# Hybrid decoder step on Trainium2: in the samples' update, the next step's broadcast values are loaded ahead of the state two steps on

## The chip, the cores and the metric

The kernel runs on one core of one Trainium2 chip. Times are device microseconds (us) from the first to the last work of one execution. The engines are TensorE (PE), VectorE (DVE), ScalarE (ACT), GpSimd (POOL) and SyncE (SP). Here POOL does little but issue DMA transfers.

## The reference

One inference step of one layer: a prompt of 256 tokens and 8 samples of one token each, 264 columns in all, model width 2048. The input projection feeds three branches (spatial gating, HGRN2, GLA), which are gated, merged and projected back; a squared-ReLU MLP of width 8192 follows. What matters here is the recurrence of HGRN2 (8 heads, state 128x128) and GLA (4 heads, state 128x256):

```
def gated_linear_recurrence(q, k, v, log_f, s0):
    """S_t = diag(f_t) S_{t-1} + k_t v_t^T ; o_t = S_t^T q_t (per head)."""
    ...
    o = einsum('bhts,bshv->bthv', att, vc) + einsum('bthd,bhdv->bthv', qc * exp(b), S)
    S = exp(b_last)[..., None] * S + einsum('bshd,bshv->bhdv', kc * exp(b_last[:, None] - b), vc)
```

For a sample there is one token: its state comes from DRAM (s0), is scaled by f, gets k v^T added, is multiplied by q, and goes back to DRAM as an output.

## The kernel before

The big products run on PE all the time. The work is cut into granules of 24 matmuls of 128x264 (`granule`): for each of 8 pairs of weight tile and columns, L602 (high part of the weights by high part of the activations), L603 (high by low) and L604 (low by high). The weights come by SP in pieces of 512 KB; ACT casts them to the high part `whi` (L109), DVE subtracts to get the low part `wlo` (L106). Five granules are loaded ahead and two are split ahead. L1296 is an epilogue of such products on DVE.

After each granule `background()` advances a counter `now` and pumps two queues of generators, which write the rest of the layer in small steps between the granules: the mixers of the prompt (`mixer_r`), the updates of the samples (`samples_r`), and others. PE and POOL execute in the order in which this is written. The order of ACT and DVE is set by a scheduler, from the order written and its costs.

`slot()` writes small 32-column matmuls to PE in one entry between two granules: levels of the prompt's recurrence (L633), the samples' output products (L640), and rounds of the conditioning's products (L342). It takes all samples that have waited long enough.

`samples_r(G)` runs for three groups: HGRN heads 0 to 3 (8 steps, one a sample), HGRN heads 4 to 7 (8 steps), and GLA (16 steps, two a sample). In a step

- `fetch` (L1029) has POOL issue the DMA of a state tile `st` (256 KB; 4 buffers). It is called two steps ahead and held back until few enough states are in use; on the chip it also waits until L640 has read the buffer's last content and the write-out L1058 is done.
- `values` (L1035) has POOL issue a broadcast of the step's v rows from the scratch `vs_d` in DRAM (filled by L1086) to all partitions, tile `vbc` (256 KB; 2 buffers). It is called one step ahead.
- ACT scales the state's heads (L1055), DVE adds k times the values (L1057), POOL writes the state out (L1058), and the step is handed to `slot()`, where PE multiplies the state by q (L640; the result `sm` is added to `os`).

A step's work is written when `now` is at least 3 granules past its fetch and 2 past its values (`FETCHED` is 3).

Around it stands `mixer_r` of the same group: L1163 (ACT, an exponential) and L100 (DVE, by q) make `qd`, L1165 makes `kd`, L1176 multiplies the two on PE, L1188 transposes `kd` on PE, L1189 copies the result by ACT to `kt`, L1197 and L1198 multiply that by v on PE, L1201 scales the result and L1203 writes it out by POOL; L1220, L1222 and L1223 make outputs on PE, L1225, L1228 and L1234 treat them on ACT, and L1243 transposes them on PE.

Of the kernel before, what the change touches and what calls it, by code (L numbers as in the profile page):

```python
# [57 lines left out]
def hybrid_step_kernel(  # L58
# [27 lines left out]
    def blk(shape=None, dt=F32):  # L86
        shape = shape or [P, 4, NT]
        return blkp.tile(shape, dt, tag="b", name=nm("b"))
# [4 lines left out]
    def tmp(shape, tag, bufs=2):  # L93
        return tp.tile(shape, F32, tag=tag, name=nm(tag), bufs=bufs)
# [4 lines left out]
    def mul(o, a, b):  # L99
        V.tensor_tensor(o, a, b, op=ALU.mult)  # L100
# [72 lines left out]
    def rstd_small(ms, scale, out):  # L173

        n, w = out.shape
        xx, aa = tmp([P, 16], "sx")[0:n, 0:w], tmp([P, 16], "sa")[0:n, 0:w]
        c = 0
        for m in ms if isinstance(ms, list) else [ms]:
            V.tensor_scalar(xx[:, c:c + m.shape[1]], m, scale, EPS, ALU.mult, ALU.add)
            c += m.shape[1]  # L180
        V.tensor_scalar(out.bitcast(I32), xx.bitcast(I32), -0.5, 1597463007.0, ALU.mult, ALU.add)
        for _ in range(3):
            mul(aa, out, out)
            V.scalar_tensor_tensor(aa, aa, -0.5, xx, ALU.mult, ALU.mult)
            V.scalar_tensor_tensor(out, aa, 1.5, out, ALU.add, ALU.mult)
# [828 lines left out]
    def samples_r(G):  # L1014

        dv = G.dv
        nj, nh = dv // P, 512 // dv
        q, k, g = G.q, G.k, G.g
        fs = tmp([P, 4, NS], "fs")
        S.activation(fs, g[:, :, NP:NT], AF.Exp)  # L1020
        qm = blk([P, 4, NS, 32])
        mul(qm, q[:, :, NP:NT].unsqueeze(3).to_broadcast([P, 4, NS, 32]),
            delta.rearrange("p (b c) -> p b c", b=NS).unsqueeze(1).to_broadcast([P, 4, NS, 32]))
        steps = [(b, h) for b in range(NS) for h in range(0, 4, nh)]
        ahead, vals = [], []

        def fetch(b, h):
            st = tmp([P, nh, dv], "st", ST_BUFS)
            nc.gpsimd.dma_start(st, G.s_in(b, h, nh))  # L1029
            ahead.append((st, now[0]))  # L1030

        def values(b, h):
            v = tmp([P, 4, P], "vbc", VB_BUFS)
            r0 = 4 * nj * b + h * nj
            nc.gpsimd.dma_start(v, vs_d[G.i, r0:r0 + 4, :].partition_broadcast(P))  # L1035
            vals.append((v.rearrange("p (h j) v -> p h (j v)", h=nh), now[0]))

        for s in steps[0:2]:
            fetch(*s)
            yield  # L1040
        values(*steps[0])
        yield
        os_ = tmp([P, dv], f"os{G.i}", 1)
        sts = []
        for n, (b, h0) in enumerate(steps):
            if n + 2 < len(steps):

                yield lambda: len(sts) + sum(len(x[3]) for x in samples) <= ST_BUFS - 3
                fetch(*steps[n + 2])
            if n + 1 < len(steps):  # L1050
                values(*steps[n + 1])
            yield lambda: now[0] >= max(ahead[0][1] + FETCHED, vals[0][1] + FETCHED - 1)
            st, v = ahead.pop(0)[0], vals.pop(0)[0]
            for i in range(nh):
                S.activation(st[:, i, :], st[:, i, :], AF.Copy, scale=fs[:, h0 + i, b:b + 1])  # L1055
            for i in range(nh):
                V.scalar_tensor_tensor(st[:, i, :], v[:, i, :], k[:, h0 + i, NP + b:NP + b + 1], st[:, i, :], ALU.mult, ALU.add)  # L1057
            nc.gpsimd.dma_start(G.s_out(b, h0, nh), st)  # L1058
            sts.append(st)
            if h0 + nh == 4:  # L1060
                samples.append((now[0], (G, qm, os_), b, sts))
                sts = []
            yield
        yield lambda: not samples
        yield READY
        ss, rr = tmp([P, 1], "sss", 1), tmp([P, 1], "srr", 1)
        S.activation(tmp([P, dv], "vt"), os_, AF.Square, accum_out=ss)
        rstd_small(ss, 1.0 / dv, rr)
        S.activation(os_, os_, AF.Copy, scale=rr)
        G.os = os_  # L1070
        yield

    def mixer_r(G):
# [18 lines left out]
        q, k, g = G.q, G.k, G.g  # L1092

        bs.g.append(samples_r(G))


# [333 lines left out]
    for m in range(7):  # L1430
        if m in PRE_AT:
            n = N_PRE // len(PRE_AT)
# [387 lines left out]
```

## Time and profile before

| | |
|---|---|
| median of 3 runs | 1940.19 us (1938.92 to 1940.46) |
| profiled execution | 1938.0 us, span 1935.8 us |
| mean granted PE clock | 0.995 |
| PE busy | 1900.1 us, 98% of the span |
| DVE busy | 1188.7 us, 61% |
| ACT busy | 1005.7 us, 52% |
| POOL busy | 88.0 us, 5% |
| DMA | 442.06 MB, mean 228 GB/s |

A row of a group gives line, engine, operation, output <- inputs, shapes and count. A row of the waits reads "who waited <- for whom: us in total, times, longest us". A row of the timeline gives start and length in us, then the instruction, and in brackets how long its engine had been idle before it and what ended that. A matmul's length overlaps that of the next, so the pace of PE is read from the starts. A row of the windows gives the busy time of each engine in a stretch, and the clock that PE was granted in it (1.00 is full speed). The three groups of samples lie at about 380 to 520, 520 to 660 and 660 to 860 us.

### The profile page before, as it was taken

The page shows a single profiled execution, that of the slowest core. Times are in us where ns is not written, and L with a number is a line of the kernel's source. Part 1 is how long each engine was busy: PE and PEld are TensorE (multiplying, and loading weights), DVE is VectorE, ACT ScalarE, POOL GpSimd, SP SyncE. Part 2 cuts the span into 40 slices and gives each one's busy share as a digit, 9 for nine tenths or more (in the row PEclk, how much of TensorE's full clock was granted, in tenths as well). Part 3 has the DMA queues.
Part 4 walks back from the last instruction along what each step waited for, and adds up shares of the span by engine and source line. Part 5 has one row for each costly group of instructions (what it writes and reads, how often), then busy time and mean ns, then how long its engine had stood idle before and what let it go on. Part 6 is the DMA issues. An engine that isn't in the chain of part 4 may idle for free. (4 is left out here: it accounts for less than half of the span.)

```text
span 1935.8 us, 42323 instructions
## 1 busy us (share of the span) xinstructions
PE 1900.1 (98%) x17072; PEld 1810.3 (94%) x17072; DVE 1188.7 (61%) x2114; ACT 1005.7 (52%) x1827; POOL 88.0 (5%) x144
## 2 busy tenths in 40 slices
PE   6999999999999999999999999999999999999998
PEld 5989999998999998999999989999999999999997
DVE  4566667686577695565555666545556555555565
ACT  5444354665666765544444566454444545454444
POOL 1000000001101112200000010000000000000000
PEclk9999999999999999999999999999999999999999
DMA  9897787688588788987777846776565555555552
GB/s 314 299 341 250 246 285 216 212 259 277 182 268 280 220 261 277 312 262 250 253 256 231 304 138 191 226 243 191 180 184 178 184 179 181 183 178 185 179 181 100
DMA packets 339381, 442.06 MB, mean 228 GB/s; under 512 B 14931, under 2 KB 281025, under 8 KB 339185
## 3 DMA queue, kind: packets, MB, share of 16 engines
q1 hardware_dynamic: 329120, 409.62, 65.5%
q0 software_dynamic: 8992, 28.48, 4.6%
q8 instruction: 134, 2.20, 0.4%
q10 hardware_dynamic: 1072, 1.25, 0.2%
q14 instruction: 63, 0.51, 0.1%
HBM read 427.60 MB, written 11.70 MB: 227 GB/s over the span
## 5 line engine op out<-in xcount | busy, mean ns | idle before, releaser
L602 PE MATMUL mm<-b,whi 128*128 128x264 f32 x4592 | 1317.2, 287 | 7.6 <-ACT b L109 3.5
L603 PE MATMUL mm<-b,whi 128*128 128x264 f32 x4592 | 1308.6, 285 | 1.9 <-DVE b L106 1.0
L604 PE MATMUL mm<-b,wlo 128*128 128x264 f32 x4592 | 1305.3, 284 | 0.3 <-DVE wlo L106 0.2
L106 DVE TENSOR_TENSOR wlo<-raw,whi 128x512 fp32r<-128x512 f32 x1136 | 776.0, 690 | 570.0 <-ACT whi L109 567.4
L109 ACT CAST whi<-raw 128x512 fp32r<-128x512 f32 x1134 | 693.9, 618 | 726.7 <-PE mm L603 647.9
L602 PEld LDWEIGHTS mm<-b,whi 128*128 128x128 f32 x4592 | 865.8, 189 | 50.2 <-issue 23.8
L603 PEld LDWEIGHTS mm<-b,whi 128*128 128x128 f32 x4592 | 865.8, 189 | 2.6 <-DVE b L106 1.1
L604 PEld LDWEIGHTS mm<-b,wlo 128*128 128x128 f32 x4592 | 866.3, 189 | 1.4 <-DVE wlo L106 0.9
L103 DVE TENSOR_TENSOR b<-b,mm 128x528 f32<-128x528 f32 (+1 forms) x137 | 95.6, 699 | 42.3 <-PE mm L604 42.3
L1057 DVE SCALAR_TENSOR_TENSOR st<-vbc,b,st 128x128 f32<-128x128 f32 (+1 forms) x96 | 34.2, 391 | 52.3 <-DMA vbc<-vs_d 46.8
L1055 ACT ACTIVATE st<-st,fs 128x128 f32<-128x128 f32 (+1 forms) x96 | 37.0, 430 | 51.3 <-DMA st<-in_state_hgrn_dram 26.0
L274 PE MATMUL ada<-b,cT 128*32 128x256 f32 (+1 forms) x640 | 35.4, 361 | 7.4 <-DMA b<-in_w_ada_dram 7.3
L342 PE MATMUL ada<-araw,cT 128*32 128x512 f32 x296 | 39.9, 601 | 0.0
L274 PEld LDWEIGHTS ada<-b,cT 128*32 128x32 f32 x640 | 18.3, 116 | 19.5 <-issue 6.8
L100 DVE TENSOR_TENSOR b<-b,b 128x512 f32<-128x512 f32 (+1 forms) x47 | 34.2, 742 | 1.4 <-ACT b L1165 0.9
L1058 POOL DMA_DIRECT2D out_dram<-st x32 | 23.5, 735 | 153.1 <-DVE st L1057 152.3
L342 PE MATMUL ada<-b,cT 128*32 128x512 f32 x216 | 25.8, 593 | 0.0
L106 DVE TENSOR_TENSOR b<-gt,b 128x528 fp32r<-128x528 f32 x32 | 22.7, 709 | 3.7 <-ACT whi L109 0.5
L106 DVE TENSOR_TENSOR b<-b 128x1024 f32<-128x1024 f32 (+1 forms) x24 | 24.4, 1018 | 0.0
L109 ACT CAST whi<-araw 128x512 fp32r<-128x512 f32 x20 | 12.4, 621 | 20.6 <-PE mm L603 18.1
L100 DVE TENSOR_TENSOR gt<-vt 128x528 f32<-128x528 f32 x32 | 22.4, 701 | 0.9 <-ACT vt L1679 0.9
L1685 ACT ACTIVATE b<-vt 128x528 fp32r<-128x528 f32 x32 | 20.7, 647 | 1.0
(374 smaller groups left out, 872.0 us busy)
## 6 DMA issues: line engine op xcount, KB each, us to landing
raw<-in_w_in_dram SPq DMA_DIRECT2D x232, 512.0 KB, 4.6
raw<-in_w_mlp_up_dram SPq DMA_DIRECT2D x128, 512.0 KB, 3.7
raw<-in_w_mlp_down_dram SPq DMA_DIRECT2D x128, 512.0 KB, 3.6
b<-in_w_ada_dram SPq DMA_DIRECT2D x102, 512.0 KB, 6.5
araw<-in_w_ada_dram SPq DMA_DIRECT2D x74, 512.0 KB, 5.4
raw<-in_w_branch_dram SPq DMA_DIRECT2D x48, 512.0 KB, 4.4
raw<-in_w_out_dram SPq DMA_DIRECT2D x32, 512.0 KB, 4.1
b<-in_w_ada_dram SPq DMA_DIRECT2D x32, 256.0 KB, 5.9
```

The source lines that it names most:

```text
L100: V.tensor_tensor(o, a, b, op=ALU.mult)
L103: V.tensor_tensor(o, a, b, op=ALU.add)
L106: V.tensor_tensor(o, a, b, op=ALU.subtract)
L109: S.copy(hi, src)
L274: T.matmul(acc[32 * j:32 * j + 32, 0:n], cT[:, k, :], w[:, n * j:n * j + n], start=k == 0, stop=k == KT - 1)
L342: T.matmul(self.acc[32 * j:32 * j + 32, :], cT[:, k, :], ws[j // 2][:, j % 2 * 512:j % 2 * 512 + 512], start=k == 0, stop=k == KT - 1)
L602: T.matmul(o, a, xh(k + j), start=first and j == 0, stop=False)
L603: T.matmul(o, a, xl(k + j), start=False, stop=False)
L604: T.matmul(o, b, xh(k + j), start=False, stop=last and j == n - 1)
L1055: S.activation(st[:, i, :], st[:, i, :], AF.Copy, scale=fs[:, h0 + i, b:b + 1])
L1057: V.scalar_tensor_tensor(st[:, i, :], v[:, i, :], k[:, h0 + i, NP + b:NP + b + 1], st[:, i, :], ALU.mult, ALU.add)
L1058: nc.gpsimd.dma_start(G.s_out(b, h0, nh), st)
```

## The change

In each step of `samples_r`, the call of `values` for the next step is made ahead of the condition that holds back the fetch, and ahead of the fetch; before, it was made behind both.

```
         for n, (b, h0) in enumerate(steps):
+            if n + 1 < len(steps):
+                values(*steps[n + 1])
             if n + 2 < len(steps):
 
                 yield lambda: len(sts) + sum(len(x[3]) for x in samples) <= ST_BUFS - 3
                 fetch(*steps[n + 2])
-            if n + 1 < len(steps):
-                values(*steps[n + 1])
             yield lambda: now[0] >= max(ahead[0][1] + FETCHED, vals[0][1] + FETCHED - 1)
```

On POOL this is the end of the first group. Names are tiles with numbers: st are the states of steps 4 to 7 (fetched here: before 5842, 5855, 6097 and after 5844, 5857, 6099 are steps 5, 6 and 7), vbc the values.

```order
-L1029 DMA st_5842<-in_state_hgrn_dram 128x4x128
-L1035 DMA vbc_5844<-vs_d 128x512
-L1058 DMA out_dram<-st_5455 128x4x128
-L1029 DMA st_5855<-in_state_hgrn_dram 128x4x128
-L1035 DMA vbc_5857<-vs_d 128x512
-L1058 DMA out_dram<-st_5602 128x4x128
-L1029 DMA st_6097<-in_state_hgrn_dram 128x4x128
-L1035 DMA vbc_6099<-vs_d 128x512
-L1058 DMA out_dram<-st_5842 128x4x128
 L1035 DMA vbc_6110<-vs_d 128x512
```
```order
+L1035 DMA vbc_5683<-vs_d 128x512
+L1029 DMA st_5844<-in_state_hgrn_dram 128x4x128
+L1058 DMA out_dram<-st_5457 128x4x128
+L1035 DMA vbc_5855<-vs_d 128x512
+L1029 DMA st_5857<-in_state_hgrn_dram 128x4x128
+L1058 DMA out_dram<-st_5604 128x4x128
+L1035 DMA vbc_5950<-vs_d 128x512
+L1029 DMA st_6099<-in_state_hgrn_dram 128x4x128
+L1058 DMA out_dram<-st_5844 128x4x128
 L1035 DMA vbc_6110<-vs_d 128x512
```

Each vbc issue has moved ahead of the st issue before it, so a step's values now precede the fetch of the state one step later. The last one, vbc_6110 of step 7, has no fetch to pass and keeps its place behind the write-out of step 5.

On DVE this is the stretch that ends with the L100 for which L1176 of the first group waits. Before (st_5855 is step 6, st_6097 is step 7):

```order
L100 TENSOR_TENSOR b_6088<-b_6088,b_4812 128x1024
L106 TENSOR_TENSOR wlo_6079<-raw_5937,whi_6078 128x512
L1057 SCALAR_TENSOR_TENSOR st_5855<-vbc_6099,b_4812,st_5855 128x128 x3
L106 TENSOR_TENSOR wlo_6083<-raw_5937,whi_6082 128x512
L1057 SCALAR_TENSOR_TENSOR st_5855<-vbc_6099,b_4812,st_5855 128x128
L1057 SCALAR_TENSOR_TENSOR st_6097<-vbc_6110,b_4812,st_6097 128x128 x2
L106 TENSOR_TENSOR wlo_6141<-raw_5982,whi_6140 128x512
L1057 SCALAR_TENSOR_TENSOR st_6097<-vbc_6110,b_4812,st_6097 128x128
L1296 SCALAR_TENSOR_TENSOR b_5863<-gt_6051,mm_6053 128x528
L106 TENSOR_TENSOR wlo_6145<-raw_5982,whi_6144 128x512
L1057 SCALAR_TENSOR_TENSOR st_6097<-vbc_6110,b_4812,st_6097 128x128
L106 TENSOR_TENSOR wlo_6177<-raw_6016,whi_6176 128x512
```

After (st_6099 is step 7; b_6091 in L100 is `qd`):

```order
L100 TENSOR_TENSOR b_6090<-b_6090,b_4812 128x1024
L106 TENSOR_TENSOR wlo_6081<-raw_5946,whi_6080 128x512
L1057 SCALAR_TENSOR_TENSOR st_6099<-vbc_6110,b_4812,st_6099 128x128 x2
L106 TENSOR_TENSOR wlo_6085<-raw_5946,whi_6084 128x512
L1057 SCALAR_TENSOR_TENSOR st_6099<-vbc_6110,b_4812,st_6099 128x128 x2
L106 TENSOR_TENSOR wlo_6150<-raw_5984,whi_6149 128x512
L100 TENSOR_TENSOR b_6091<-b_6091,b_170 128x512
L1296 SCALAR_TENSOR_TENSOR b_5872<-gt_6053,mm_6055 128x528
```

Step 6's adds have moved up (they stand further ahead now), and one L106 and the L1296 no longer stand between step 7's first add and the L100 of `qd`, which before follows the last row shown.

On PE the samples' products of steps 5 and 6 of the first group are now in one entry. After:

```order
L604 MATMUL mm_6160<-b_1274,wlo_6085 128x264
L633 MATMUL sm_6245<-b_5909 32x64 x16
L640 MATMUL sm_6262<-st_5844,b_5016 32x128
L640 MATMUL sm_6262<-st_5857,b_5016 32x128
L640 MATMUL sm_6262<-st_5844,b_5016 32x128
```

Before, the entry behind L633 holds step 5 alone (st_5842), step 6 has the next entry with L1188 and L342, and step 7 one of its own later. In the whole program PE has three entries with 32-column matmuls fewer; the number of matmuls is the same.

On ACT, in the third group, the copies to `kt`. Before:

```order
L109 CAST whi_10110<-raw_9957 128x512
L109 CAST whi_10114<-raw_9957 128x512
L1189 COPY b_10124<-sm_10125 128x512
L1189 COPY b_10124<-sm_10131 128x512
L109 CAST whi_10161<-raw_10013 128x512
```

After (st_10096 and st_10152 are steps 8 and 9):

```order
L1189 COPY b_10089<-sm_10090 128x512
L1055 ACTIVATE st_10096<-st_10096,fs_9007 128x256
L1055 ACTIVATE st_10152<-st_10152,fs_9007 128x256
L109 CAST whi_10134<-raw_9973 128x512
L1055 ACTIVATE st_10152<-st_10152,fs_9007 128x256
L109 CAST whi_10138<-raw_9973 128x512
L1189 COPY b_10089<-sm_10144 128x512
```

The scaling of two more states has moved in between the two copies. In this group PE's entries with L640 stand up to 8 granules earlier than before, the last one behind granule 219 instead of 227.

More of the change, by code (lines that the diff above doesn't have):

```diff
@@ L1045, in samples_r @@
         for n, (b, h0) in enumerate(steps):
+            if n + 1 < len(steps):
+                values(*steps[n + 1])
             if n + 2 < len(steps):
@@ L1049, in samples_r @@
                 fetch(*steps[n + 2])
-            if n + 1 < len(steps):
-                values(*steps[n + 1])
             yield lambda: now[0] >= max(ahead[0][1] + FETCHED, vals[0][1] + FETCHED - 1)
```

## The prediction

> **What bounds the kernel now.** I read the totals of the page first, then the list of waits, then PE's own waits in the stretch where the samples are updated, then the timeline around the one wait found there.
>
> ```profile
> span 1935.8 us, 42323 instructions
> PE 1900.1 (98%) x17072; PEld 1810.3 (94%) x17072; DVE 1188.7 (61%) x2114; ACT 1005.7 (52%) x1827; POOL 88.0 (5%) x144
> ...
> POOL st L1029 <- PE sm L640: 132.3, 12, 17.8
> ...
> DVE st L1057 <- DMA vbc<-vs_d: 46.8, 18, 5.9
> ...
> ACT st L1055 <- DMA st<-in_state_gla_dram: 25.0, 10, 6.8
> ```
>
> PE is busy for 98% of the span, so a wait costs time only where PE ends up idle. The waits that the change aims at are long (DVE waited 18 times for broadcast values, 46.8 us), but DVE is busy 61% and ACT 52%. How much of them reaches PE is told by PE's waits from 380 to 520 us (first HGRN group) and by its busy time per stretch (columns: stretch, length, PE, PEld, DVE, ACT and POOL busy, granted clock, DMA share, GB/s; the last row sums 380 to 860 us, all three groups):
>
> ```profile
> PE sm L1176 <- DVE b L100: 3.8, 1, 3.8
> PE mm L604 <- DVE wlo L106: 0.2, 1, 0.2
> ...
> 380.00:520.00 140.00, 136.01 (x1526) 125.23 (x1519) 94.14 (x188) 87.99 (x190) 14.56 (x22) 0.99 0.77 249
> ...
> sum 480.00, PE 475.62 PEld 442.88 DVE 328.04 ACT 302.86 POOL 66.86; mean PE 118.91 PEld 110.72 DVE 82.01 ACT 75.71 POOL 16.71
> ```
>
> In those 480 us PE is idle 480.00 − 475.62 = 4.38 us, and 3.99 of it lies in the first group: nearly all one wait, L1176 for L100. That is the only place where the 46.8 us can be seen on the path, and the whole gain has to come from there and from how PE's pieces are cut. Its surroundings:
>
> ```profile
> 478.77 1.16 PE L1176 MATMUL sm<-b,b 128*128 128x128 f32 x8 [3.76 <-DVE b L100]
> ...
> 480.57 0.42 PE L604 MATMUL mm<-b,wlo 128*128 128x264 f32 x1
> ...
> 483.21 0.42 PE L604 MATMUL mm<-b,wlo 128*128 128x264 f32 x1
> ...
> 483.73 0.29 PE L604 MATMUL mm<-b,wlo 128*128 128x264 f32 x1
> ...
> 484.10 0.28 PE L604 MATMUL mm<-b,wlo 128*128 128x264 f32 x1
> ```
> ```profile
> 474.37 0.61 DVE L1057 SCALAR_TENSOR_TENSOR st<-vbc,b,st 128x128 f32<-128x128 f32 x2 [0.35 <-DMA vbc<-vs_d]
> 474.90 0.69 DVE L106 TENSOR_TENSOR wlo<-raw,whi 128x512 fp32r<-128x512 f32 x1
> 475.50 0.34 DVE L1057 SCALAR_TENSOR_TENSOR st<-vbc,b,st 128x128 f32<-128x128 f32 x1
> 475.77 0.70 DVE L1296 SCALAR_TENSOR_TENSOR b<-gt,mm 128x528 f32<-128x528 f32 x1
> 476.38 0.68 DVE L106 TENSOR_TENSOR wlo<-raw,whi 128x512 fp32r<-128x512 f32 x1
> 476.98 0.34 DVE L1057 SCALAR_TENSOR_TENSOR st<-vbc,b,st 128x128 f32<-128x128 f32 x1
> 477.25 0.68 DVE L106 TENSOR_TENSOR wlo<-raw,whi 128x512 fp32r<-128x512 f32 x1
> 478.03 0.69 DVE L100 TENSOR_TENSOR b<-b,b 128x512 f32<-128x512 f32 x1
> ```
> ```profile
> 477.36 0.63 ACT L1163 ACTIVATE b<-b 128x512 f32<-128x512 f32 x1 [1.87 <-DVE st L1057]
> ```
>
> Read backwards: PE (idle from 478.77 − 3.76 = 475.01) waits for L100, L100 for the exponential L1163, L1163 for the last add L1057 of the group's last step, and the first of those adds waited for its broadcast values until 474.37. The values left POOL last in a burst of four:
>
> ```profile
> 465.48 0.75 POOL L1029 DMA_DIRECT2D st<-in_state_hgrn_dram  x1 [0.21 <-PE sm L640]
> 466.22 0.55 POOL L1035 DMA_DIRECT2D vbc<-vs_d  x1
> 466.76 0.76 POOL L1058 DMA_DIRECT2D out_dram<-st  x1
> 467.51 0.55 POOL L1035 DMA_DIRECT2D vbc<-vs_d  x1
> ```
>
> Issued at 467.51, they were used at 474.37, 6.86 us later.
>
> **The change part by part.** It swaps two issues on POOL in 6 of the 8 steps of each HGRN group and 14 of the 16 of the GLA group; nothing is added or dropped, and POOL is busy 88 us in all, so issuing itself costs nothing. The values no longer stand behind the fetch that waits for a state buffer (132.3 us of waits for PE's L640, above). The price is that each fetch is issued one values issue later, 0.55 us. No new blocking: the buffer of the next values needs the adds of the step before last, and the write-out just ahead on POOL already waits for those.
>
> *The stall at L1176.* The values of the last step keep their place, behind the write-out of step 5. But those of step 6 leave the burst, being issued a wave earlier; step 7's are then third of three. The fetch still waits for L640 of step 3, which stands in the same row of PE, so the issues are at 465.48, 466.2 and 467.0: 0.52 us earlier (467.51 − 466.99). Fewer transfers lie ahead; step 6's, second in its burst, landed within 6.07 us, from 466.22 to the add that did not wait for it:
>
> ```profile
> 472.29 0.87 DVE L1057 SCALAR_TENSOR_TENSOR st<-vbc,b,st 128x128 f32<-128x128 f32 x3
> ```
>
> With that, the last values are there at 466.99 + 6.07 = 473.1, that is 1.3 us earlier. Behind them DVE's order is shorter: one L106 (476.38) and the L1296 (475.77) no longer stand between the last adds and L1163, 0.60 + 0.61 = 1.2 us by their start-to-start times. Together −2.5; the stall shrinks from 3.76 to about 1.2. Bounds: −1.2 (only the order) and −3.76 (all of it). I take −2.5.
>
> *The clock behind it.* The granted clock falls in stretches of 3.41 us:
>
> ```profile
> 104.66:108.07 3.41, 1.39 (x12) 1.20 (x11) 3.37 (x9) 1.97 (x4) 0.00 (x0) 1.00 0.80 253
> 108.07:111.48 3.41, 3.41 (x18) 3.41 (x17) 2.11 (x8) 1.78 (x3) 0.00 (x0) 0.50 1.04 392
> ```
> ```profile
> 473.30:476.71 3.41, 1.71 (x15) 1.50 (x13) 3.06 (x8) 1.08 (x2) 0.76 (x1) 1.00 1.07 403
> 476.71:480.12 3.41, 1.35 (x11) 1.35 (x12) 2.51 (x5) 1.24 (x3) 0.76 (x1) 1.00 1.04 393
> 480.12:483.54 3.42, 3.42 (x18) 3.42 (x17) 0.69 (x1) 1.11 (x2) 0.00 (x0) 0.50 0.90 329
> ```
>
> Where PE was busy 1.39 or 1.35 of 3.41 us, the next stretch ran at clock 0.50; after 1.71 it did not. At half clock twelve matmuls took 483.21 − 480.57 = 2.64 us, 0.22 each; at full clock three took 484.10 − 483.73 = 0.37, 0.123 each. 3.42 / 0.22 = 15.5 matmuls, each 0.097 late: 1.5 us. A stall that ends near 476.2 leaves 476.71 to 480.12 busy, so I take −1.5 (bounds 0 and −1.5; the stretches may lie otherwise in other executions). The Trainium skill, "TensorE: Matmul & The Clock Gate", section "Why this matters for your kernels", asks for no PE-idle gaps over about 3 us. By it a residual stall of up to 3 us would be free of the clock's loss; by the stretch from 104.66, where 3.41 − 1.39 = 2.02 us of idleness was enough, it would not. The 3.76 us agree with the rule, the 2.02 us don't, and the measurement decides; at 1.2 us both give −1.5.
>
> *PE's pieces.* The products L640 of two steps now go to PE in one entry more often: three entries with 32-column matmuls fewer, the same matmuls. What entering and leaving costs:
>
> ```profile
> 784.87 0.28 PE L604 MATMUL mm<-b,wlo 128*128 128x264 f32 x1
> 785.08 0.64 PE L640 MATMUL sm<-st,b 128*32 128x256 f32 x8
> 785.65 0.39 PE L602 MATMUL mm<-b,whi 128*128 128x264 f32 x1
> 785.88 0.28 PE L603 MATMUL mm<-b,whi 128*128 128x264 f32 x1
> ```
>
> 785.08 − 784.87 = 0.21 and 785.88 − 785.65 = 0.23 against 0.12 inside the stream: 0.2 us an entry, −0.6 for three. Bounds 0 and, if the whole 785.88 − 784.87 − 0.24 = 0.77 went, −2.3.
>
> *The third group.* Its steps come closer together (L640 entries up to 8 granules earlier), so states are fetched sooner after their buffers come free and ACT, which scales them, has less slack. One place touches PE: the copy L1189 that L1198 needs stands behind step 9's L1055 now. Such a state took this long before:
>
> ```profile
> 803.11 0.72 POOL L1029 DMA_DIRECT2D st<-in_state_gla_dram  x1 [8.32 <-PE sm L640]
> ```
> ```profile
> 809.56 0.91 ACT L1055 ACTIVATE st<-st,fs 128x256 f32<-128x256 f32 x2 [6.79 <-DMA st<-in_state_gla_dram]
> ```
> ```profile
> DMA to landing us min/median/max: 3.0/5.7/9.5
> ```
>
> That is 6.45 us from issue to use, and ACT's 6.79 us there cost PE nothing; over all states (last row) the slowest took 9.5. The new place is in no row of before. Bounds: −0.4, all that PE idles outside the first group (4.38 − 3.99), and +4.5, if a state lands at 9.5 instead of 6.45, L1198 waits all of the 3.0 us between and the clock's 1.5 go too. The median of 5.7 lies below the 6.45 that cost nothing, so I take a value near the lower end, +0.2. The 0.2 us at L604 above, behind a late L106, goes: −0.2.
>
> Sum: −2.5 − 1.5 − 0.6 + 0.2 − 0.2 = −4.6 us. The profiled execution took 1938.0 us (span 1935.8 plus 2.2), so the profile after should read about 1933.4; the median of the runs, 1940.19, lies 2.2 above it, and 1940.19 − 4.6 = 1935.6.
>
> **The rivals.**
> 1. *The third group gives it back*: step 9's state lands late, L1198 waits up to those 3.0 us and the clock may fall. For it: ACT waited 10 times, up to 6.8 us, for these states. Against: none of those waits reached PE. Instead of +0.2 there stand +3.0 or +4.5: −1.8 or −0.3, 1938.4 to 1939.9.
> 2. *The stall stays*, because the values of the last step are not moved ahead of any fetch: they land as late as before, some 6.9 us after issue, or L1163 has another wait in its place, so that only order and pieces gain, and the clock still falls: −0.6 for the pieces alone to −1.2 − 0.6 = −1.8: 1938.4 to 1939.6. For it: the row at 467.51 stands in the same place in both programs; against: the burst ahead of it gets shorter.
> 3. *Slower*: each fetch stands 0.55 us later behind a 256 KB broadcast, and in the third group six pairs of steps follow on one another more tightly. If states then land towards 9.5 us after issue, ACT stands in L1055 with the casts L109 of the weights behind it, and PE starves once a pair. It decides from 1.5 us a pair, half of the 3.0 above: 6 × 1.5 = 9.0, less 4.6, is +4.4: 1944.6. Against: before, ACT stood still for 6.79 us without a gap on PE.
>
> The Trainium skill, "SBUF — State Buffer", section "SBUF: two separate sides", warns that DMAs issued from POOL starve for descriptors while DVE runs some of its operations; that would work towards rival 3, as DVE's work gets denser. The four issues at 465.48 to 467.51 took 0.55 to 0.76 us each in a busy stretch; no row shows one held up.
>
> **How the numbers follow.** My forecast has 0.60 (own range 1932.6, the larger bounds of pieces and stall, to 1937.5), rival 1 0.17, rival 2 0.13, rival 3 0.10. A measurement of this kernel tells about 0.2%, 3.9 us, from no change, so faster means below 1936.3. Of the forecast's 0.60 I put 0.46 below that; 0.02 of rival 1 too: faster 0.48. The rest of the forecast, of rival 1 and rival 2 give 0.42 for the same; slower 0.10. The range from 1932.6 to 1941.0 leaves out rival 3 and as much again for costs that no row bounds.
>
> **What would show it.** PE's wait at L1176 of the first group near 1.2 us, at most 2.5; no stretch at clock 0.50 behind it; DVE's waits for the values well under 46.8 us, most of this without effect; the last values issued about 467.0 and used by 473.1; PE idle from 660 to 860 us still under 0.5 us. Wrong, if L1176 still waits over 3 us, or if L1198, L1220 or L1243 wait on ACT, or L602 to L604 on L109 or L106, in the third group.

## The result, and the profile after

The changed kernel is slower by 0.3%: 1947.05 us (median of 18 runs) against 1940.63 us for the kernel before (18 runs). The ratio is 1.0029, 95% interval 1.0020 to 1.0038; of 1940 us that is +5.6 us (+3.9 to +7.4). It is not the ratio of the medians, and it leaves out one slow run of the kernel before, of 2063.71 us. Below, each ratio is turned into us in the same way. The profiled execution took 1948.27 us, 1.2 above its median; the one of before, 1938.0, lay 2.6 below its own, so the two profiles lie further apart than the kernels do.

The page and the waits of the changed kernel:

```profile
span 1946.0 us, 42329 instructions
PE 1904.0 (98%) x17072; PEld 1812.8 (93%) x17072; DVE 1189.5 (61%) x2113; ACT 1004.1 (52%) x1827; POOL 87.7 (5%) x144
...
DVE st L1057 <- DMA vbc<-vs_d: 32.7, 13, 5.8
```

The change did what it says to the wait it is aimed at: DVE waited 32.7 us for values instead of 46.8. PE, however, now waits in all three groups (its waits from 380 to 520, from 520 to 660 and from 660 to 860 us, and then the sum row of the windows 380 to 520, 520 to 660 and 660 to 865 us):

```profile
PE sm L1176 <- DVE b L100: 1.9, 1, 1.9
PE mm L604 <- DVE wlo L106: 0.9, 1, 0.9
...
PE sm L633 <- DVE b L100: 2.1, 1, 2.1
PE mm L604 <- DVE wlo L106: 1.0, 1, 1.0
...
PE sm L1198 <- ACT b L1189: 2.1, 1, 2.1
PE sm L1243 <- ACT b L1245: 1.2, 1, 1.2
PE mm L604 <- DVE wlo L106: 0.9, 1, 0.9
...
sum 485.00, PE 473.91 PEld 440.08 DVE 325.98 ACT 297.55 POOL 66.11; mean PE 157.97 PEld 146.69 DVE 108.66 ACT 99.18 POOL 22.04
```

PE is idle 485.00 − 473.91 = 11.09 us there, against 4.38 before. One wait was halved and six came in its place. I lined the two executions up by the start of every 24th big matmul. The first group then gained 1.0 us, the second lost 5.2 and the third 7.0. That is one pair of executions; the experiments give each group by itself.

**First group, its start.** The values of the fourth step were issued at 411.20, and DVE was there long before they landed (POOL, DVE and PE, in the timeline):

```profile
411.20 0.55 POOL L1035 DMA_DIRECT2D vbc<-vs_d  x1
...
419.88 1.14 DVE L1057 SCALAR_TENSOR_TENSOR st<-vbc,b,st 128x128 f32<-128x128 f32 x4 [1.56 <-DMA vbc<-vs_d]
420.94 0.68 DVE L106 TENSOR_TENSOR wlo<-raw,whi 128x512 fp32r<-128x512 f32 x1
...
421.67 0.39 PE L604 MATMUL mm<-b,wlo 128*128 128x264 f32 x1 [0.90 <-DVE wlo L106]
```

DVE stands 1.56 us for values issued 8.68 us before, does four adds, and only then the low part that PE needs. In DVE's order of before, these adds stood a whole wave later, and the same low part followed on the last add of the third step:

```profile
418.42 0.34 DVE L1057 SCALAR_TENSOR_TENSOR st<-vbc,b,st 128x128 f32<-128x128 f32 x1
418.68 0.69 DVE L106 TENSOR_TENSOR wlo<-raw,whi 128x512 fp32r<-128x512 f32 x1
```

The scheduler has put the fourth step's adds ahead of `wlo` because their DMA now stands earlier on POOL: with the order of the DMAs changed alone (the first experiment below) they stand there too, and with the writing times changed alone they do not.

**First group, L1176.** (POOL, ACT, DVE, PE, then the busy time and the clock of two stretches.)

```profile
467.42 0.55 POOL L1035 DMA_DIRECT2D vbc<-vs_d  x1
...
472.51 1.12 ACT L109 CAST whi<-raw 128x512 fp32r<-128x512 f32 x2
...
474.21 0.61 DVE L1057 SCALAR_TENSOR_TENSOR st<-vbc,b,st 128x128 f32<-128x128 f32 x2 [1.44 <-ACT whi L109]
...
477.39 1.16 PE L1176 MATMUL sm<-b,b 128*128 128x128 f32 x8 [1.93 <-DVE b L100]
...
475.13:478.55 3.42, 1.50 (x13) 1.28 (x13) 3.32 (x8) 2.18 (x4) 0.76 (x1) 1.00 1.03 396
478.55:481.96 3.41, 3.41 (x19) 3.41 (x18) 1.69 (x4) 1.20 (x2) 0.00 (x0) 0.51 0.87 278
```

The stall fell from 3.76 to 1.93 us. The last values were again used 6.8 us after their issue (467.42 to 474.21). The row names L109 as what ended DVE's wait, but those casts were done at 473.63; by the trace the values landed at 474.13, so it was they. And 1.93 us of idleness was enough for half clock in the next stretch (0.51).

**Second group.** Before, PE did not wait here. Now the adds of step 4 wait on DVE for values that left POOL 9.3 us earlier, and an L100 that the level products L633 need stands behind them; half clock follows (POOL, DVE, PE and the clock after, then DVE before):

```profile
579.53 0.55 POOL L1035 DMA_DIRECT2D vbc<-vs_d  x1
...
588.83 0.35 DVE L1057 SCALAR_TENSOR_TENSOR st<-vbc,b,st 128x128 f32<-128x128 f32 x1 [5.82 <-DMA vbc<-vs_d]
...
591.04 0.95 PE L633 MATMUL sm<-b 128*32 128x32 f32 x64 [2.14 <-DVE b L100]
...
591.26:594.68 3.42, 3.42 (x81) 3.04 (x68) 3.42 (x8) 0.00 (x0) 1.04 (x2) 0.50 0.71 178
```
```profile
585.59 0.62 DVE L1057 SCALAR_TENSOR_TENSOR st<-vbc,b,st 128x128 f32<-128x128 f32 x2 [1.80 <-DMA vbc<-vs_d]
```

Before, the adds of step 3 stood at this place and waited 1.80 us, for values that had left POOL second in their burst, behind a fetch alone. The values of step 4, which are needed there now, leave third, behind a fetch and a write-out: 9.3 us from issue to use instead of 6.5 (579.12 to 585.59).

**Third group.** The steps come earlier, so state 9 is fetched at 750.03. Its scaling stands on ACT ahead of the second copy L1189, for which PE's L1198 waits:

```profile
750.03 0.70 POOL L1029 DMA_DIRECT2D st<-in_state_gla_dram  x1
...
758.47 0.51 ACT L1055 ACTIVATE st<-st,fs 128x256 f32<-128x256 f32 x1 [2.31 <-DMA st<-in_state_gla_dram]
...
760.31 0.57 ACT L1189 COPY b<-sm 128x512 f32<-128x512 f32 x1
...
760.94 0.70 PE L1198 MATMUL sm<-b,b 128*128 128x256 f32 x2 [2.07 <-ACT b L1189]
...
762.02:765.44 3.42, 3.42 (x16) 3.25 (x15) 2.54 (x5) 0.91 (x3) 0.58 (x1) 0.51 0.82 238
...
805.95 0.66 PE L1243 MATMUL sm<-cst,b 128*128 128x128 f32 x4 [1.25 <-ACT b L1245]
```

State 9 landed about 8.4 us after its issue (750.03 to 758.47). In the kernel before the two copies stood together and waited for no state:

```profile
749.61 1.07 ACT L1189 COPY b<-sm 128x512 f32<-128x512 f32 x2
```

### The profile page after: what moved, and what is told of

Same layout as the page of the kernel before. It is cut to its first block, busy times and chain, and to the rows that moved or that the text cites. A ratio compares the mean times of both kernels' runs of the same rounds, so it can differ in the third digit from the quotient of the medians.

```text
span 1946.0 us, 42329 instructions
## 1 busy us (share of the span) xinstructions
PE 1904.0 (98%) x17072; PEld 1812.8 (93%) x17072; DVE 1189.5 (61%) x2113; ACT 1004.1 (52%) x1827; POOL 87.7 (5%) x144
## 5 line engine op out<-in xcount | busy, mean ns | idle before, releaser
L604 PE MATMUL mm<-b,wlo 128*128 128x264 f32 x4592 | 1306.6, 285 | 3.0 <-DVE wlo L106 2.8
L106 DVE TENSOR_TENSOR wlo<-raw,whi 128x512 fp32r<-128x512 f32 x1136 | 777.0, 690 | 588.3 <-ACT whi L109 586.0
L109 ACT CAST whi<-raw 128x512 fp32r<-128x512 f32 x1134 | 693.1, 618 | 727.6 <-PE mm L603 651.8
L604 PEld LDWEIGHTS mm<-b,wlo 128*128 128x128 f32 x4592 | 867.1, 189 | 5.1 <-DVE wlo L106 4.5
L1057 DVE SCALAR_TENSOR_TENSOR st<-vbc,b,st 128x128 f32<-128x128 f32 (+1 forms) x96 | 33.9, 391 | 41.7 <-DMA vbc<-vs_d 32.7
L342 PE MATMUL ada<-araw,cT 128*32 128x512 f32 x296 | 40.9, 600 | 0.2 <-DMA araw<-in_w_ada_dram 0.2
L274 PEld LDWEIGHTS ada<-b,cT 128*32 128x32 f32 x640 | 18.4, 116 | 19.0 <-issue 6.8
L100 DVE TENSOR_TENSOR b<-b,b 128x512 f32<-128x512 f32 (+1 forms) x47 | 34.1, 743 | 1.2 <-ACT b L1165 0.9
L342 PE MATMUL ada<-b,cT 128*32 128x512 f32 x216 | 27.5, 627 | 0.0
L106 DVE TENSOR_TENSOR b<-gt,b 128x528 fp32r<-128x528 f32 x32 | 22.7, 708 | 3.4
L106 DVE TENSOR_TENSOR b<-b 128x1024 f32<-128x1024 f32 (+1 forms) x24 | 24.4, 1019 | 0.0
L109 ACT CAST whi<-araw 128x512 fp32r<-128x512 f32 x20 | 12.4, 622 | 20.9 <-PE mm L603 19.1
L100 DVE TENSOR_TENSOR gt<-vt 128x528 f32<-128x528 f32 x32 | 22.4, 701 | 0.9 <-ACT vt L1679 0.9
L342 PEld LDWEIGHTS ada<-b,cT 128*32 128x32 f32 x216 | 7.2, 114 | 16.4 <-issue 16.0
```

The lines of the kernel that those rows point to most:

```text
L106: V.tensor_tensor(o, a, b, op=ALU.subtract)
L109: S.copy(hi, src)
L274: T.matmul(acc[32 * j:32 * j + 32, 0:n], cT[:, k, :], w[:, n * j:n * j + n], start=k == 0, stop=k == KT - 1)
L342: T.matmul(self.acc[32 * j:32 * j + 32, :], cT[:, k, :], ws[j // 2][:, j % 2 * 512:j % 2 * 512 + 512], start=k == 0, stop=k == KT - 1)
L604: T.matmul(o, b, xh(k + j), start=False, stop=last and j == n - 1)
```

## The experiments

The change does two things at once. It changes the order of the DMAs on POOL, and it changes when a step's work is written: the rule "3 granules after the fetch of the state, 2 after the values" was bound by the values, and these are now issued before the hold. In the edits below, `ahead_of` selects the steps whose values go ahead of the fetch; where it is false the order is that of before. Line numbers in the experiments are shifted by a few (L1057 is then L1059, L1060 or L1062, and so on).

### Order and pace taken apart, all groups

The order alone (the DMAs of after, the writing times of before), against the changed kernel:

```
                 fetch(*steps[n + 2])
+            if n + 1 < len(steps):
+                vals[-1] = (vals[-1][0], now[0])
```

> The DMAs stand as in the changed kernel, but a step's work (scaling, adds, products) is written at the granule at which the kernel before writes it: the time of the values' issue is taken where it was before, behind the fetch. PE's pieces stand as before. Theory A (most of the loss comes from the steps being written up to some granules earlier, so that their instructions stand in ACT's and DVE's order before their data has landed): the waits of the third group (L1198, L1243) and the 2.1 us at L633 of the second are gone, the three waits of 0.9 to 1.0 us of L604 at the start of each group stay, since DVE's adds of the fourth step still stand there, and L1176 still gains 1.8: between -1 and +3 us against the kernel before. Rival B (the transfers' order alone costs: a state issued behind a broadcast lands later): as the changed kernel, +5 to +7 us.

Measured: 1.0034 (1.0021 to 1.0046), +6.6 us.

The pace alone (the DMAs of before, the writing times of after), against the kernel before:

```
+            seen = now[0]
             if n + 2 < len(steps):
...
                 values(*steps[n + 1])
+                vals[-1] = (vals[-1][0], seen)
```

> The DMAs stand in the order of the kernel before, but a step's work is written as early as in the changed kernel: the time of the values' issue is taken ahead of the hold. PE's pieces stand as in the changed kernel. Theory A: +3 to +5 us against the kernel before; L1198 and L1243 of the third group wait 1 to 2 us each, L1176 of the first group still waits about 3.8 us, and L604 does not wait at the start of the groups. Rival B: within 1 us of the kernel before.

Measured: 1.0043 (1.0029 to 1.0057), +8.3 us. Neither theory held for both: the order alone came out where rival B had it, the pace alone above both. By the point values each half alone costs no less than both together, so they are not two terms of a sum. On the waits theory A was mostly right. With the order alone there was none at L1198 and L1243, but the 2.0 us at L633, which it saw gone, stayed, and L604 waited 1.2 us in the second and the third group and only 0.2 in the first; with the pace alone L1198 and L1243 waited 1.7 and 2.0 us and L1176 3.9 us.

Lined up with the kernel before by the big matmuls, as above, these two profiled executions split by group: the order alone gained 2.6 us in the first group and lost 4.6 in the second and 1.8 in the third; the pace alone lost 0.5, 0.2 and 8.5. So the gain at L1176 (2.0 us of wait with the order alone) and the loss of the second group go with the order, and most of the loss of the third group with the pace. Each is one execution.

### One group at a time

```
+            ahead_of = G.i < 2      # or: G.i == 2, G.i == 1, G.i == 0
```

> The change in the two HGRN groups alone, the GLA group as before. From the drift between the two profiled executions (+1.4 at the start of the first group, -2.3 around L1176, +1.3 and +3.7 in the second) theory A gives +2 to +4 us. A rival C, that all of the loss sits in the third group, gives -2 to 0.

Measured: 1.0001 (0.9992 to 1.0009), +0.2 us (−1.6 to +1.7): below theory A's 2 to 4, at the edge of rival C's −2 to 0.

> The change in the GLA group alone. From the drift (+1.5 at its start, and some +5 to +6 from L1198 on): theory A gives +3 to +6 us; rival C +6 to +8, all of the loss and the gain of the first group missing too; if the loss were in the HGRN groups, 0 to +1.

Measured: 1.0026 (1.0016 to 1.0036), +5.0 us, of about 5.6 in all, as theory A had it and less than rival C. In its profiled execution L1198 waits 1.4 us and L1243 1.3, and no stretch of the clock halves there, so some 2.7 of the 5.0 us are named and the rest is not. So the third group holds nearly all of the net loss. That the HGRN groups net nothing is no sign that nothing happens there:

> The change in the second HGRN group alone. If the HGRN groups' loss sits here: L604 waits 0.9 to 1.2 us at the group's start and L633 waits 1.6 to 2.1 us for L100, behind adds that wait for values: +3 to +5 us against the kernel before. Rival (the loss sits at the start of the first group): +1 to +1.5 us, the wait of L604 alone.

Measured: 1.0020 (1.0011 to 1.0029), +3.9 us, with the two waits expected, one of them longer:

```profile
PE mm L604 <- DVE wlo L106: 2.2, 1, 2.2
PE sm L633 <- DVE b L100: 1.7, 1, 1.7
```

> The change in the first HGRN group alone, from its first step on. It differs from the run of the group's tail by the values of steps 1 to 3 alone. If the second group holds the loss: -3 to -5 us, the gain of the tail less the wait of L604 at the start. Rival: -1 to +1 us, the start taking back what the tail brings.

Measured: 0.9979 (0.9970 to 0.9988), −4.1 us. First, second and third group give −4.1 + 3.9 + 5.0 = +4.8 us, inside the interval of the whole (+3.9 to +7.4): the account closes by group. That the first group's −4.1 is near the −4.6 of the forecast is luck: in its profiled execution L1176 still waited 2.0 us and a stretch at half clock followed, so of the forecast's terms the clock's did not come and the stall's came in part.

### Order and pace in the third group

The same two edits as above, for `G.i == 2` alone.

> In the GLA group alone: the DMAs in the changed order, a step's work written at the granule at which the kernel before writes it. Theory A in the third group (its loss comes from steps written earlier: L1198 and L1243 behind the scaling of states that have not landed, and the rounds L342 shifted): no wait at L1198 and L1243, at most the wait of about 1 us of L604 seen in the run with the DMA order alone: 0 to +2 us against the kernel before. Rival B: the +4.9 us of the GLA group come from the DMA order: +4 to +6.

Measured: 1.0004 (0.9996 to 1.0012), +0.8 us.

> In the GLA group alone: the DMAs in the order of the kernel before, but a step's work written as early as in the changed kernel. Theory A: L1198 and L1243 wait 1 to 2 us each: +4 to +8 us against the kernel before (the run with this in all groups gave +8.3). Rival B: within 1 us of it.

Measured: 1.0044 (1.0030 to 1.0058), +8.5 us. PE's waits from 660 to 870 us:

```profile
PE sm L1246 <- ACT b L1248: 2.9, 1, 2.9
PE sm L1201 <- ACT b L1192: 2.1, 1, 2.1
PE sm L640 <- DVE st L1060: 1.3, 2, 0.9
```

(L1243 for L1245, L1198 for L1189, and L640 for the adds, in the numbering of before.) Here theory A holds, slightly above its range: in the third group the order alone costs nothing that can be told from zero, and the pace alone is enough for the whole loss. The values moved ahead may even repay some of it (8.5 against 5.0 with both, but the intervals overlap).

### Removing one of the two stalls of the third group

On top of the change in the GLA group alone, no step is written between the copies `kt` and the write-out L1203:

```
-            yield lambda: now[0] >= max(...)
+            yield lambda: not (still[0] and G.i == 2) and now[0] >= max(...)
...
+        still[0] = G.i == 2
         kt = blk([P, 2, 512])
...
+        still[0] = False
         ss = tmp([P, 8], "ss", 1)
```

> The change in the GLA group alone, as in the run with that group alone, but no sample's step is written while the mixer's state products (from the transposes L1188 to the write-out L1203) are written. Step 9's scaling then stands behind these on ACT. Theory A: L1198 no longer waits 1.4 us for L1189, and +4.9 us of that run go down to +2 to +3.5; L1243 may still wait. Rival B (the transfers' order costs, wherever the step is written): still +4 to +6.

Measured: 1.0040 (1.0028 to 1.0053), +7.8 us. L1198 waited no more, as expected, but the time did not fall:

```profile
PE sm L1249 <- ACT b L1251: 2.2, 1, 2.2
...
PE sm L1249 <- ACT b L1240: 0.6, 1, 0.6
```

The steps held back came in a bunch behind, and L1243 (here L1249) waited 2.2 + 0.6 us instead of 1.3, with a stretch at half clock behind it; L604 waited 1.3 us for DVE at 826 us, which it did not without the hold. Removing one stall moved the loss to the next places where PE needs ACT or DVE. That it grew is not shown: the interval, +5.4 to +10.3, overlaps that of the group alone, +3.1 to +7.0.

### Single moves

```
+            ahead_of = G.i == 0 and n == 5
```

> One DMA alone is moved: in the first group the values of the step before the last (step 6) go ahead of the fetch of the last state. Theory D (the gain of the changed kernel at L1176 comes from this one move, because the scheduler then puts step 6's adds further ahead in DVE's order): L1176 waits about 1.9 us instead of 3.8, L604 does not wait at the start of the groups, L1198, L1243 and L633 don't wait: -2 to -3.5 us against the kernel before. Rival (each DMA moved contributes its part): within 1 us of the kernel before, with L1176 still over 3 us.

Measured: 1.0009 (1.0001 to 1.0018), +1.7 us. Theory D fell: L1176 did not wait less. It waited 4.8 us, against 3.5 to 4.7 in the six traces whose first group is that of before.

```profile
467.54 0.55 POOL L1035 DMA_DIRECT2D vbc<-vs_d  x1
...
473.88 1.14 DVE L1060 SCALAR_TENSOR_TENSOR st<-vbc,b,st 128x128 f32<-128x128 f32 x4 [4.52 <-issue]
...
PE sm L1179 <- DVE b L100: 4.8, 1, 4.8
```

Step 6's values are issued at 467.54, no earlier than before, since they stand behind a write-out that waits for step 4's adds. But their adds have moved up in DVE's order, and stop DVE for 4.5 us (the trace names no releaser; 473.88 is 6.3 us after the issue). The exponentials, L100 and L1176 are late with them. So this one move does not bring the gain at L1176; moving the values of steps 4 and 5 with it does (below). Which of these two is needed was not run.

> Two DMAs alone are moved: in each HGRN group the values of the fourth step (step 3) go ahead of the fetch of the fifth state. Theory D: DVE's four adds of step 3 then stand ahead of the low parts wlo that PE needs next, and wait there for values issued only just before; L604 waits about 1 us at the start of each of the two groups, all else is as before: +2 to +3 us against the kernel before, the two drifts of 1.3 of the changed kernel. Rival (the waits of L604 at the starts come from the values of the second and third steps, or from DMAs crowding each other): within 1 us of the kernel before, no wait of L604 over 0.5 us there.

The edit is `ahead_of = G.i < 2 and n == 2`. Measured: 1.0007 (0.9998 to 1.0015), +1.4 us, not told apart from zero. L604 waited 0.8 us at the start of the second group, near what was expected, and 0.4 in all in the first, less than the 0.9 of the changed kernel. In the second group L604 waits in no trace where that group is as before, so that one moved DMA makes the wait there is shown, in one execution; for the first group it is not.

> As the kernel with one DMA moved, and in the first group the write-out of step 5 also goes behind the values of the last step, so that these stand second in their burst on POOL, 0.76 us earlier. If the rest of the stall at L1176 is the landing of these values: L1176 waits 0.8 to 1.4 us and the stretch at half clock behind it is gone: -3 to -5 us against the kernel before, 1 to 2 us better than with the one DMA alone. Rival (the rest is the DVE and ACT chain behind, or the transfer lands when the queue lets it): L1176 still waits 1.9 us, and the time is that of the kernel with one DMA moved.

On top of `G.i == 0 and n == 5`, the write-out of step 5 is issued behind the last values. Measured: 1.0004 (0.9995 to 1.0013), +0.8 us, L1176 waiting 4.8 us as in the run that it builds on, so it could not tell what it was made for.

### A version that keeps the gain

```
+            ahead_of = G.i == 0 and n >= 3
```

> The change in the first group alone and from its fourth step on (the values of steps 4, 5 and 6 move ahead of the fetches of states 5, 6 and 7), all else as before. By now the reading is: a values DMA that is moved takes its adds with it in DVE's order, and that pays only if the values then land before DVE gets there. Here step 4's values are issued behind the write-out of step 2, some 16 us ahead of where they were, and step 6's some 15 us: all land before their adds. So L1176 waits about 1.9 us instead of 3.8 as in the changed kernel, and no L604 waits at the group's start: -1 to -3 us against the kernel before. Rival (DVE's adds at a new place cost elsewhere as much as they bring): within 1 us, with new waits of L604 or L602 of about 1 us in the first group.

Measured: 0.9973 (0.9964 to 0.9983), −5.2 us, more than expected. The values of step 6 leave POOL at 451.12, 13.4 us before their adds, and these wait for nothing:

```profile
451.12 0.55 POOL L1035 DMA_DIRECT2D vbc<-vs_d  x1
...
464.53 1.13 DVE L1060 SCALAR_TENSOR_TENSOR st<-vbc,b,st 128x128 f32<-128x128 f32 x4
...
PE sm L1179 <- DVE b L100: 2.5, 1, 2.5
PE mm L604 <- DVE wlo L106: 0.2, 1, 0.2
...
473.27:476.68 3.41, 1.59 (x14) 1.38 (x12) 2.42 (x7) 0.74 (x2) 0.48 (x1) 1.00 1.05 404
476.68:480.10 3.42, 2.75 (x23) 2.75 (x24) 3.04 (x5) 2.25 (x5) 0.28 (x1) 1.00 0.88 309
```

In the profiled execution L1176 still waited 2.5 us, but 1.82 of them (3.41 − 1.59) lay in one clock stretch and the rest in the next, and the clock did not fall there. (The stretches are counted back from the next one at half clock, which begins at 831.67.) Then the write-out of step 5 as well goes behind the last values:

```
+            ahead_of = G.i == 0 and 3 <= n < 6
...
+            if G.i == 0 and n == 6:
+                nc.gpsimd.dma_start(G.s_out(*steps[5], nh), st)
...
-            nc.gpsimd.dma_start(G.s_out(b, h0, nh), st)
+            if not (G.i == 0 and n == 5):
+                nc.gpsimd.dma_start(G.s_out(b, h0, nh), st)
```

> As the run before it, and the write-out of step 5 goes behind the values of the last step, so that these leave POOL second in their burst, 0.76 us earlier. If their landing sets the rest of the stall: L1176 waits 0.8 to 1.4 us, no stretch at half clock follows, -2.5 to -4.5 us against the kernel before. Rival (the transfer lands when the queues let it, whatever its place): L1176 still near 1.9 us and the time of the run before it.

Measured: 0.9963 (0.9951 to 0.9974), −7.2 us; 1933.79 us, median of 5 runs, against 1940.56. It beats both kernels, by more than expected. The intervals of the last two runs overlap, so what moving the write-out adds is seen in the trace and not told apart in the time.

```profile
466.95 0.55 POOL L1035 DMA_DIRECT2D vbc<-vs_d  x1
...
472.98 0.88 DVE L1062 SCALAR_TENSOR_TENSOR st<-vbc,b,st 128x128 f32<-128x128 f32 x3
...
476.17 1.16 PE L1182 MATMUL sm<-b,b 128*128 128x128 f32 x8 [0.43 <-DVE b L100]
```

The last values were used 6.0 us after their issue without a wait, the stall is 0.43 us, and PE has no stretch at half clock between 111 and 1919 us.

## Why the prediction was wrong, point by point

- **What bounds the kernel** was read rightly: of the waits for values, only the one ahead of L1176 reached PE in the trace of before, and 14 us less of these waits (46.8 to 32.7) came with more idle time of PE, not less.
- **The stall at L1176**: −2.5 forecast, 3.76 to 1.93, −1.8, in the profiled execution. The half by DVE's shorter order came: from the first add to L1176 it takes 3.18 us (474.21 to 477.39) instead of 4.40 (474.37 to 478.77). Of the rest, 0.45 us is no gain: PE came to L1176 later (475.46 instead of 475.01). The half by an earlier landing did not: the last values left at 467.42, not 467.0, and took 6.8 us again instead of 6.07.
- **The clock**: −1.5 forecast, nothing came: half clock still follows L1176, and the stalls in the second and the third group brought a stretch of it each. The Trainium skill ("TensorE: Matmul & The Clock Gate", section "Why this matters for your kernels") sets its limit at PE-idle gaps of about 3 us; here 1.93 us in one stretch halved the clock, so the measurement again decides against that figure. That the forecast let a 1.2 us stall pass was no error of the rule but of the stall's size.
- **PE's pieces**: −0.6 forecast. No run changes them alone, so this stays open.
- **The late L106**: −0.2 forecast, and the opposite came: L604 waits 0.9 to 1.0 us early in each group. The failed step here, and for the second group, is the sentence "No new blocking". It looked at POOL and at buffers. It did not follow the moved values to their adds, which DVE's scheduler moves ahead with them, in front of low parts that PE needs. The order of DVE's instructions that I showed for one place near L1176 held the same fact for the starts, and I did not read it there.
- **The second group** had no term at all; by itself it costs +3.9 us, by the same oversight: there the moved adds hold up the L100 that L633 needs.
- **The third group**: +0.2 forecast, +5.0 measured. This is the step that was mis-sized most. The place was named rightly, L1198 behind L1189 behind step 9's scaling, and so was the bound of the wait, 3.0 us, of which 2.07 came, with half clock behind. What failed is the choice near the lower end on the strength of the median landing (its 5.7 counts the write-outs too; the fetches alone have 5.6): state 9 needed 8.4 us, and of two states that stood in the way it was the later one that counted. L1243 was listed only as something to look for. PE idle from 660 to 860 us, which was to stay under 0.5 us, came to 4.51 (200.00 − 195.49).
- **The rivals**: rival 1 named the mechanism and put it at 1938.4 to 1939.9, one stall and one clock loss set against a gain of 4.6 us. Its mechanism decided, but it stopped 7 us short of the measured time: the gain it was set against was not there once the second group and the starts are counted. Rival 3 expected six pairs of steps to starve PE through the casts L109; the measured loss is instead a few places where PE needs a single result of ACT or DVE. Rival 2 was half right: the landing did stay. The warning on DMAs from POOL ("SBUF — State Buffer", section "SBUF: two separate sides" of the Trainium skill) does not show in the issues: those in the rows above took 0.55 to 0.70 us, no longer than before. Whether it has a part in the landings, which came later (last section), no run here tells.

## What to carry to other kernels

Here a load that was moved ahead took its consumers with it, in the scheduler's order and in the rule that times work by the issue of a load. Such a move pays only where the load's landing moves by more than the consumer does, so compare the distance from issue to first use, in the new order, with the landing times in the trace, for each in-order engine, and look at what else stands behind the consumer there. A change that is applied everywhere through a loop is best costed place by place: here the same swap was worth −4.1, +3.9 and +5.0 us in three groups, and −7.2 us when it was kept to the tail of the first group, where PE had waited, and the last write-out went behind the last values.

## What the runs showed of the hardware that I had not expected

- The clock halves after less idleness than I had assumed: PE busy 1.50 of 3.42 us in a stretch (1.92 idle) was enough; 1.71 of 3.41 (1.70 idle) in the trace of before was not. A stall of 2.5 us that lay across two stretches did not halve it.
- Idle time as the profile counts it is not the whole rule. In the run with the tail of the first group, 1.82 us idle in a stretch did not halve the clock at 476.68, and 1.72 did at 831.67. In the changed kernel a stretch with PE busy 2.87 us, from 1155.20 on with matmuls of 1 to 128 columns, was followed by half clock. What the clock goes by is not shown.

```profile
1154.49:1157.90 3.41, 2.87 (x28) 2.65 (x30) 1.93 (x13) 1.98 (x8) 0.00 (x0) 1.00 0.00 0
1157.90:1161.31 3.41, 3.41 (x20) 0.85 (x16) 3.05 (x20) 2.48 (x8) 2.04 (x4) 0.50 0.00 0
```

- The transfers took longer with the order changed. The median landing of the values rose from 6.5 to 7.1 us and that of the fetched states from 5.6 to 5.9 (values before and after, then states before and after; from one execution each, and why is not shown):

```profile
DMA to landing us min/median/max: 3.8/6.5/9.6
...
DMA to landing us min/median/max: 4.8/7.1/10.0
...
DMA to landing us min/median/max: 3.0/5.6/9.5
...
DMA to landing us min/median/max: 3.5/5.9/10.1
```
